# A hybrid attention and gated-MLP encoder layer: the rounded factors of w_down's first block are made among w_o's products, the first head's q and k are loaded earlier, and two pool results share one buffer

## The chip, the cores and the metric

The kernel runs on one core of a Trainium2 chip. The metric is the device time of one execution in microseconds (us): the median of the timed runs. A profiled execution beside them gives the trace; its span is a little shorter than its own time, since what lies around the first and the last instruction is not in it.

## The reference, cut to what matters

One layer over 512 tokens of width 2048, in float32. A combined projection gives q, k, v (eight heads of 128) and u (1024 channels for pooling); attention looks at its own chunk of 64 tokens and the eight before it, so with 512 tokens at everything up to the own chunk; the pool is a trailing mean minus the token, then a linear map per group. Then w_o, a residual, and a gated MLP with a depthwise causal convolution of three taps.

```python
h = rms_norm(x, pre_mix_g)
z = h @ w_in                                  # q | k | v | u
a = chunked_attention(q, k, v, rel_bias)
p = multiscale_pool(u, pool_w, pool_scale)    # windows 2, 4, 8, 16
x = x + rms_norm(concat(a, p) @ w_o, post_mix_g)
h = rms_norm(x, pre_ffn_g)
up = causal_dwconv(h @ w_up, conv_w, conv_b)
y = (gelu(up[..., :D_FF]) * up[..., D_FF:]) @ w_down   # D_FF = 5632
x = x + rms_norm(y, post_ffn_g)
```

## The kernel before, in words

**Split products.** TensorE multiplies rounded numbers (`fp32r`), so each float32 factor is split in two: ACT writes the rounded part (`hi`, line 140 or 143), DVE the rest (`lo = src - hi`, line 141 or 144). `split` does both. A product is then two or three matmuls (`mm3`, lines 162, 164, 165; `mm2`, lines 170 and 176). A weight is loaded into a raw buffer by SP, split into a pair of `w4` buffers, and read by TensorE. There are eight `w4` buffers, four pairs, given out in turn, and five shared raw buffers (`raw4`).

**Stages, in TensorE's order.** (1) Head 0's q and k, while x arrives. (2) `v_steps(0)`: half of v. (3) The projection of q and k of heads 1 to 7: k = 0 to 6, seven products each, named i = 1, 2, 5, 3, 6, 7, 4. It is Strassen's scheme in Winograd's form, seven products of halves instead of eight. Class `Pairs` holds the order, loads raw factors (`wx`, `ww`, `wz`, `wy`, line 449) up to eight products ahead and makes the split factors (`wfh`, `wfl`) up to four ahead. Product i = 4 adds onto the PSUM bank `qa` which ACT has just copied for i = 7 (`zm`, line 582), so TensorE waits there until ACT has read it. The finished z of each head is stored to DRAM (`zqk`, line 591). (4) Attention of heads 0 to 2 among the other half of v, then heads 3 to 7 among the eight u projections with the pool; each head loads its z into `zq` and its bias (`load_z`, `load_bias`), multiplies by the norm factor and splits it (`ready_head`) before `scores`. (5) w_o, again as seven products (`WO = 1, 7, 2, 5, 6, 3, 4`), each in two column halves `cc`, each half in four quarters of one weight pair. (6) The up projection, again in seven products per block: the longest part. (7) The down projection and the end.

**Side work.** The sums of weight blocks that Strassen's scheme needs for w_o and for the first block of w_down are made in DRAM by DMAs alone: copies and accumulating adds of 1 MB each, 48 in all (`sums_in_dram`; tensors `wt` and `t`). `more_sums(n)` issues the next n of them; calls stand at fixed places in the program. A paced one waits for a `pace` memset on DVE behind the last split. Besides, three factors of w_down's first block, (column half, product) = (0, 1), (1, 1), (0, 2), are rounded long before they are needed and kept in DRAM as `ready_w`; each is done in two parts, so there are six blocks of 512 KB. `Pairs` does that: one block behind product 7 of each of k = 0 to 5.

```python
v = self.raw[k, i] = p0.tile([P, 1024], F32, tag="rw", bufs=1, name="rw")   # line 455, loaded at 456
pair = w4("rwh"), w4("rwl")                                                 # line 474
split(*pair, self.raw.pop((k, i)))                                          # line 475
self.stores = [...]                                  # line 476; issued at the next make, line 468
```

The pair comes from the same four `w4` pairs as the factors that TensorE reads.

**Order.** TensorE's instructions stay as the program writes them. Those of ACT, DVE, POOL and SP are put in order when the kernel is built, by a scheduler with its own estimate of times; on the chip each of these engines works its list in order, and a waiting instruction holds all behind it. `tc.issue_after(ins)` puts an instruction behind another. The same layer places the tiles, and puts a wait before a buffer's next use. SP keeps at most eight of its DMAs on the way.

Of the kernel before, what the change touches and what calls it, by code (L numbers as in the profile page):

```python
# [9 lines left out]
F32 = mybir.dt.float32  # L10
# [71 lines left out]
def encoder_layer(ctx: ExitStack, tc: tile.TileContext, x, xT, vecs, rel, post_mix, post_ffn,  # L82
# [349 lines left out]
    class Pairs:  # L432
# [3 lines left out]
        def __init__(self):  # L436
# [6 lines left out]
            for m in range(len(ready_parts)):  # L443
                self.order.insert(self.order.index((m, 7)) + 1, (None, m))
            self.raw, self.made, self.loaded, self.used, self.stores = {}, [], 0, 0, []

        def load(self, k, i):
# [4 lines left out]
            if k is None:  # L452
# [5 lines left out]
            elif i == 1:  # L458
# [7 lines left out]
        def make(self, k, i):  # L466
            for dest, v in self.stores:
                nc.sync.dma_start(dest, f32(v).rearrange("p (a b) -> p a b", a=2))
            self.stores = []
            if k is None:  # L470
                if i is None:
                    weights.prefetch_to(FIRST_PART + 1)
                else:
                    (cc, n), j = ready_parts[i]
# [41 lines left out]
    for n, _ in enumerate(v_steps(0, psv)):  # L516
        if n in (4, 7, 10, 13):
            more_sums(1)
# [81 lines left out]
    steps = None  # L600
    for k, i in [at for at in pairs.order if at[0] is not None]:
# [11 lines left out]
        if i in ((3, 7, 4) if 0 < k < 5 else (7, 4)):  # L613
            more_sums(1)
# [10 lines left out]
    with tc.tile_pool(name="p1", bufs=2, reuse_waits="tile") as p1:  # L625
# [11 lines left out]
        t512("bias", bufs=1)  # L637
# [9 lines left out]

        state = {}
# [130 lines left out]
        load_z(0)  # L779
# [964 lines left out]
```

## Time and profile before

| | |
|---|---|
| median of 3 runs | 1921.48 us (1920.15 to 1921.66) |
| profiled execution | 1921.59 us, span 1919.8 us |
| busy, share of the span | PE 98%, PEld 83%, DVE 80%, ACT 56%, POOL 16% |
| HBM | 370.35 MB read, 104.33 MB written |
| DMA queues, share of 16 engines | q0 (POOL's) 44.8%, q1 (SP's) 37.9% |

A row of a timeline gives the start, the duration, the engine, the line, the operation, the tiles `out<-in`, and in brackets how long the engine had been idle before it and what ended that. A row of a table of waits gives who waited for whom, the total in us, how often, and the longest. A row of the chain of waits gives start, duration and what ran there. The DMA share is the mean busy share of the 16 DMA engines.

### The profile page before, as it was taken

What the parts mean: (1) busy time and instruction counts of PE and PEld (TensorE: products, weight loads), DVE (VectorE), ACT (ScalarE), POOL (GpSimd) and SP (SyncE); (2) the same over time, 40 slices, a digit from 0 to 9 for tenths busy, and PEclk for the clock granted to TensorE, in tenths of its full rate; (3) what the DMA queues carried; (4) which work ended last, traced back from release to release, by engine and by line L of the source; (5) the groups of instructions that cost most, each with busy time, mean ns of one, the idle gap of its engine ahead of it and who ended that gap; (6) DMA issues with size and microseconds to landing.
All of it is one profiled execution on the core that took longest, in us unless ns stands there. A gap on an engine that the chain in (4) does not pass through costs nothing.

```text
span 1919.8 us, 25463 instructions
## 1 busy us (share of the span) xinstructions
PE 1873.3 (98%) x9598; PEld 1595.0 (83%) x9598; DVE 1539.6 (80%) x1799; ACT 1080.7 (56%) x1376; POOL 299.0 (16%) x394
## 2 busy tenths in 40 slices
PE   9987879999999999999999999999999999999998
PEld 7876768788889888888888888888888888888886
DVE  6876657778678988888887888888887799898875
ACT  8544435446546566656565656556565665565553
POOL 3211010110000121222212121222211011111111
PEclk9998989999999999999999999999999999999999
DMA  7699997779967789898988888888988977877785
GB/s 258 211 265 289 288 260 242 186 211 277 351 203 291 181 210 211 195 204 194 210 197 199 203 202 208 196 204 194 206 189 274 349 226 176 197 198 169 173 229 152
DMA packets 140026, 426.01 MB, mean 222 GB/s; under 512 B 11968, under 2 KB 15424, under 8 KB 134208
## 3 DMA queue, kind: packets, MB, share of 16 engines
q0 software_dynamic: 54528, 170.41, 44.8%
q1 hardware_dynamic: 85376, 253.98, 37.9%
q8 instruction: 75, 1.23, 0.3%
q14 instruction: 47, 0.39, 0.1%
HBM read 370.35 MB, written 104.33 MB: 247 GB/s over the span
## 4 chain that ended last, share of the span: by engine, by line
PE 90%; DMA 5%; DVE 2%; ACT 2%; issue 1%; SPq 0%; DVEq 0%; ACTq 0%; POOLq 0%
PE qa L170 17%; PE qa L176 9%; PE qg L170 9%; PE qg L176 4%; PE qd L170 4%; PE pa L162 4%; PE pa L164 4%; PE pa L165 4%; PE m L164 3%; PE m L165 3%; PE m L162 2%; PE qd L176 2%; PE pg L162 2%; PE pg L164 2%; PE pg L165 2%; PE v L162 1%
## 5 line engine op out<-in xcount | busy, mean ns | idle before, releaser
L141 DVE TENSOR_TENSOR wfl<-wx,wfh 128x1024 fp32r<-128x1024 f32 x192 | 234.8, 1223 | 93.8 <-ACT wfh L140 70.5
L140 ACT ACTIVATE wfh<-wx 128x1024 fp32r<-128x1024 f32 x192 | 203.4, 1059 | 180.5 <-PE qg L170 50.7
L170 PE MATMUL qa<-gT,wfh 128*128 128x512 f32 x1152 | 295.7, 399 | 0.0
L170 PEld LDWEIGHTS qa<-gT,wfh 128*128 128x128 f32 x1152 | 212.1, 193 | 39.1
L176 PE MATMUL qa<-gT,wfl 128*128 128x256 f32 x1152 | 165.7, 288 | 21.8 <-ACT zm L582 21.4
L1361 POOL DMA_DIRECT2D wx<-in_w_up x122 | 104.5, 857 | 499.7 <-DVE wfl L141 476.8
L176 PEld LDWEIGHTS qa<-gT,wfl 128*128 128x128 f32 x1152 | 154.4, 194 | 27.8 <-ACT zm L582 22.7
L170 PE MATMUL qg<-h,wfh 128*128 128x512 f32 x656 | 165.7, 394 | 0.0
L140 ACT ACTIVATE wfh<-wy 128x1024 fp32r<-128x1024 f32 x96 | 101.8, 1060 | 110.2 <-PE qg L170 60.1
L170 PEld LDWEIGHTS qg<-h,wfh 128*128 128x128 f32 x656 | 122.9, 188 | 28.0
L141 DVE TENSOR_TENSOR bl<-b,bh 128x2048 fp32r<-128x2048 f32 x56 | 127.4, 2288 | 22.8 <-ACT bh L140 11.8
L140 ACT ACTIVATE bh<-b 128x2048 fp32r<-128x2048 f32 x56 | 105.8, 1912 | 48.1 <-DVE b L1119 20.3
L141 DVE TENSOR_TENSOR wfl<-wy,wfh 128x1024 fp32r<-128x1024 f32 x96 | 117.2, 1221 | 12.2 <-ACT wfh L140 4.0
L162 PE MATMUL pa<-bh,ah 128*128 128x512 f32 x320 | 126.1, 394 | 0.0
L164 PE MATMUL pa<-bl,ah 128*128 128x512 f32 x320 | 125.8, 393 | 0.0
L165 PE MATMUL pa<-bh,al 128*128 128x512 f32 x320 | 125.5, 392 | 0.0
L141 DVE TENSOR_TENSOR wfl<-wz,wfh 128x1024 fp32r<-128x1024 f32 x48 | 58.8, 1224 | 55.4 <-PE qa L170 53.5
L170 PE MATMUL qd<-gT,wfh 128*128 128x512 f32 x384 | 95.7, 391 | 0.0
L176 PEld LDWEIGHTS qg<-h,wfl 128*128 128x128 f32 x656 | 89.4, 188 | 7.5
L176 PE MATMUL qg<-h,wfl 128*128 128x256 f32 x656 | 91.6, 282 | 0.0
L170 PEld LDWEIGHTS qd<-gT,wfh 128*128 128x128 f32 x384 | 72.0, 188 | 16.2
L170 PE MATMUL qa<-h,wfh 128*128 128x512 f32 x328 | 83.2, 395 | 0.0
(549 smaller groups left out, 4363.5 us busy)
## 6 DMA issues: line engine op xcount, KB each, us to landing
wx<-in_w_up POOLq DMA_DIRECT2D x122, 512.0 KB, 5.9
b<-in_w_down SPq DMA_DIRECT2D x32, 1024.0 KB, 6.8
wt<-in_w_o POOLq DMA_DIRECT2D x24, 1024.0 KB, 14.8
wx<-in_w_up SPq DMA_DIRECT2D x43, 512.0 KB, 5.4
wz<-in_w_up SPq DMA_DIRECT2D x41, 512.0 KB, 5.7
wy<-in_w_up SPq DMA_DIRECT2D x41, 512.0 KB, 4.6
wy<-in_w_up POOLq DMA_DIRECT2D x41, 512.0 KB, 6.7
sum<-part POOLq DMA_DIRECT2D x38, 512.0 KB, 6.3
```

Of the source, the lines that this page charges most:

```text
L140: rounded = nc.scalar.activation(hi, src, AF.Copy)
L141: rest = nc.vector.tensor_sub(lo, src, f32(hi))
L162: nc.tensor.matmul(ps, l[0], r[0], start=first, stop=False, skip_group_check=onto)
L164: nc.tensor.matmul(low, l[0], r[1], start=False, stop=False, skip_group_check=onto)
L165: nc.tensor.matmul(ps, l[1], r[0], start=False, stop=last, skip_group_check=onto)
L170: nc.tensor.matmul(ps, w[0][:, kb], pairs[kb][0], start=fresh and not kb, stop=last, skip_group_check=not fresh)
L176: nc.tensor.matmul(ps[:, sl], w[1][:, kb], pair[:, sl], start=False, stop=last, skip_group_check=not fresh)
L1361: nc.gpsimd.dma_start(self.raw[k, what], self.block(k, m, kh), accum_op=ALU.add)
```

## The change

The six blocks leave the projection. `Pairs` no longer has entries for them. A generator `ready_block` does one block during each half of the w_o products 5, 6 and 3: it loads the block at the first quarter, splits at the third and stores both parts at the fourth. Its tiles `rw` and `rwh` belong to the pool `p2` of the w_o stage, one buffer each; the lower part is written in place over the raw block.

The 48 sums are issued at other places: 6 instead of 4 in `v_steps(0)`, 20 instead of 18 in the projection, 6 instead of 5 in heads 0 to 2, 6 as before in the middle of the u projections, 5 instead of 4 behind them, 3 instead of 9 among w_o's products, and 2 as before in the up projection.

Head 0's z and bias are loaded right after `restore` (called behind product 7 of k = 6) into two `raw4` buffers, no longer when `p1` has been opened. `bias` gets two buffers, and the later loads of z and bias are put behind the loads of `restore` or behind the last weight load.

`spill_mix` gathers two pool results in one `raw4` buffer and stores both with one DMA of 512 KB; before, each went through one 256 KB buffer `mx` of its own.

```diff
@@ class Pairs
             self.order.insert(-2, (None, None))
-            for m in range(len(ready_parts)):
-                self.order.insert(self.order.index((m, 7)) + 1, (None, m))
...
-                if i is not None:
-                    (cc, n), j = ready_parts[i]
-                    v = self.raw[k, i] = p0.tile([P, 1024], F32, tag="rw", bufs=1, name="rw")
-                    nc.sync.dma_start(v.rearrange("p (a b) -> p a b", a=2),
-                                      first_block(cc, n - 1, 0)[:, 2 * j:2 * j + 2, :])
...
-            for dest, v in self.stores:
-                nc.sync.dma_start(dest, f32(v).rearrange("p (a b) -> p a b", a=2))
-            self.stores = []
...
-                    pair = w4("rwh"), w4("rwl")
-                    split(*pair, self.raw.pop((k, i)))
-                    self.stores = [(dest[:, 2 * j:2 * j + 2, :], v) for dest, v in zip(ready_w[cc, n], pair)]
@@ v_steps(0)
-        if n in (4, 7, 10, 13):
+        if n in (3, 5, 7, 9, 11, 13):
             more_sums(1)
@@ the projection's loop
         if (k, i) == (pairs.n - 1, 7):
             restore()
-        if i in ((3, 7, 4) if 0 < k < 5 else (7, 4)):
+            state["z", 0] = raw4("zq0").rearrange("p (a b) -> p a b", a=2)
+            nc.sync.dma_start(state["z", 0], zqk[0])
+            state["bias", 0] = raw4("bias0")[:, :S]
+            restore.last = nc.sync.dma_start(state["bias", 0], rel[0]).ins
+        if i in ((3, 7, 4) if k < pairs.n - 1 else (7, 4)):
             more_sums(1)
@@ attention
-        t512("bias", bufs=1)
+        t512("bias", bufs=2)
...
         def load_bias(h):
-            state["bias", h] = t512("bias", bufs=1)
-            nc.sync.dma_start(state["bias", h], rel[h])
+            state["bias", h] = t512("bias", bufs=2)
+            with tc.issue_after(restore.last):
+                nc.sync.dma_start(state["bias", h], rel[h])
 
         def load_z(h):
             state["z", h] = p1.tile([P, 2, S], F32, tag="zq", bufs=1, name="zq")
-            nc.sync.dma_start(state["z", h], zqk[h])
+            with tc.issue_after(load_w.last if h == 1 else restore.last):
+                nc.sync.dma_start(state["z", h], zqk[h])
...
         def spill_mix(kb, ps, scale):
-            v = t512("mx", bufs=1)
-            nc.scalar.activation(v, ps, AF.Copy, scale=scale)
-            nc.sync.dma_start(pooled[:, kb - HEADS, :], v)
+            if kb % 2 == 0:
+                state["mx"] = raw4("mx").rearrange("p (a b) -> p a b", a=2)
+            nc.scalar.activation(state["mx"][:, kb % 2], ps, AF.Copy, scale=scale)
+            if kb % 2:
+                nc.sync.dma_start(pooled[:, kb - 1 - HEADS:kb + 1 - HEADS, :], state.pop("mx"))
...
-        load_z(0)
-        load_bias(0)
         v_load(0)
...
-            if h:
-                more_sums(1)
+            more_sums(1)
...
-                more_sums(1 if j % 2 or not j else 0)
+                more_sums(1 if j in (0, 1, 3, 5, 6) else 0)
@@ w_o
+        def ready_block(at, j):
+            v, hi = (p2.tile([P, 1024], dt, tag=tag, name=tag) for tag, dt in (("rw", F32), ("rwh", F32R)))
+            lo = v.bitcast(F32R)
+            nc.sync.dma_start(v.rearrange("p (a b) -> p a b", a=2), first_block(at[0], at[1] - 1, 0)[:, 2 * j:2 * j + 2, :])
+            yield
+            yield
+            split(hi, lo, v)
+            yield
+            for dest, part_ in zip(ready_w[at], (hi, lo)):
+                nc.sync.dma_start(dest[:, 2 * j:2 * j + 2, :], f32(part_).rearrange("p (a b) -> p a b", a=2))
+
         def wo_product(i, cc, left, between=None):
             ps = [bank(f"m{i}{cc}{t}") for t in range(2)]
-            if cc:
-                more_sums(2 if i in (3, 6) else 1)
+            if cc and i in (1, 5, 6):
+                more_sums(1)
+            ready = ready_block(*ready_parts.pop(0)) if i in (5, 6, 3) else iter(())
             for q in range(4):
...
+                next(ready, None)
```

Each fence shows one engine's instructions in the order in which they stand in the built kernel. First ACT, which makes the rounded parts, in the projection around the end of one k and the start of the next. Before (`qa`, a PSUM bank, copied into `zm` for product 7 is the last row; `rwh` is the block's rounded part):

```order
L140 ACTIVATE wfh<-wy 128x1024
L140 ACTIVATE rwh<-rw 128x1024
L568 ACTIVATE za<-qa_1227 128x512
L140 ACTIVATE wfh<-wx 128x1024
L578 ACTIVATE zm<-qa_1036 128x512
L140 ACTIVATE wfh<-wx 128x1024
L140 ACTIVATE wfh<-wy 128x1024
L140 ACTIVATE wfh<-wx 128x1024
L582 ACTIVATE zm<-qa_1036 128x512
```

and now:

```order
L140 ACTIVATE wfh<-wy 128x1024
L140 ACTIVATE wfh<-wx 128x1024
L551 ACTIVATE za<-qa_1222 128x512
L140 ACTIVATE wfh<-wx 128x1024
L561 ACTIVATE zm<-qa_1039 128x512
L140 ACTIVATE wfh<-wy 128x1024
L140 ACTIVATE wfh<-wx 128x1024
L565 ACTIVATE zm<-qa_1039 128x512
```

The row of `rwh` is gone, and the factors behind it have moved up by one place.

Second SP, which issues the loads, at the end of the projection. Before (`zqk` are the stored heads in DRAM, `u` and `v` weights):

```order
L152 DMA v_1r<-in_w_v 128x1024
L591 DMA zqk_352<-z 128x1024
L152 DMA v_2r<-in_w_v 128x1024
L152 DMA v_3r<-in_w_v 128x1024
L152 DMA u_0r<-in_w_u 128x1024
L152 DMA u_1r<-in_w_u 128x1024
L591 DMA zqk_353<-z 128x1024
L667 DMA zq<-zqk_346 128x1024
L663 DMA bias<-in_rel 128x512
```

and now:

```order
L152 DMA v_1r<-in_w_v 128x1024
L574 DMA zqk_352<-z 128x1024
L597 DMA zq_2029<-zqk_346 128x1024
L599 DMA bias_2031<-in_rel 128x512
L649 DMA bias<-in_rel 128x512 x2
L152 DMA v_2r<-in_w_v 128x1024
L654 DMA zq<-zqk_347 128x1024
L574 DMA zqk_353<-z 128x1024
```

Head 0's load has moved up past two v weights, two u weights and the store of the last head.

Third the w_o stage, where the blocks are now. ACT before, at the end of product 2's weights and the start of product 5's (`wo_1_…` is a quarter of the second column half, `wo_0_…` of the first):

```order
L140 ACTIVATE s_4634<-mixT_3915 128x1024
L140 ACTIVATE s_4634<-mixT_3916 128x1024
L140 ACTIVATE wo_1_0h<-wo_1_0r 128x1024
L140 ACTIVATE wo_1_1h<-wo_1_1r 128x1024
L140 ACTIVATE wo_1_2h<-wo_1_2r 128x1024
L140 ACTIVATE wo_1_3h<-wo_1_3r 128x1024
L140 ACTIVATE wo_0_0h<-wo_0_0r 128x1024
```

and now:

```order
L140 ACTIVATE rwh<-rw 128x1024
L140 ACTIVATE s_4616<-mixT_3885 128x1024
L140 ACTIVATE wo_1_0h<-wo_1_0r 128x1024
L140 ACTIVATE s_4616<-mixT_3886 128x1024
L140 ACTIVATE wo_1_1h<-wo_1_1r 128x1024
L140 ACTIVATE wo_1_2h<-wo_1_2r 128x1024
L140 ACTIVATE wo_1_3h<-wo_1_3r 128x1024
L140 ACTIVATE rwh<-rw 128x1024
L140 ACTIVATE wo_0_0h<-wo_0_0r 128x1024
```

Blocks two and three stand ahead of `wo_1_0h` of product 2 and `wo_0_0h` of product 5; block four, six rows on, ahead of `wo_1_1h` of product 5. SP there, now, with what each row waits for (the rows from `wt_96` are product 5's):

```order
L846 DMA rw01l<-rw 128x1024 [waits DMAHW3_49,DMAHW1_49]
L152 DMA wo_1_1r<-in_w_o 128x2x512 [waits DMAHW2_49,DVE_49]
L840 DMA rw<-in_w_down 128x2x512 [waits DMAHW1_49]
L152 DMA wo_1_2r<-in_w_o 128x2x512 [waits DMAHW4_49,DVE_49]
L152 DMA wo_1_3r<-in_w_o 128x2x512 [waits DMAHW5_49,DVE_49]
L152 DMA wo_0_0r<-wt_96 128x1024 [waits DMAHW6_49,DMAHW7_49,DMASW4_49,DVE_49]
L846 DMA rw01h<-rwh 128x1024 [waits Activation_49]
L846 DMA rw01l<-rw 128x1024 [waits DMAHW3_49,DMAHW0_49,DVE_49]
L152 DMA wo_0_1r<-wt_96 128x1024 [waits DVE_49]
L152 DMA wo_0_2r<-wt_96 128x1024 [waits DMAHW2_49,DMASW5_49,DVE_49]
L840 DMA rw<-in_w_down 128x2x512 [waits DMAHW0_49]
L152 DMA wo_0_3r<-wt_96 128x1024 [waits DMAHW4_49,DVE_49]
```

The blocks' loads stand further ahead than the program writes them, the second already among product 2's weights. Each load but the first waits for the DMA that stored the lower part of the block before it out of the same tile (`DMAHW…`), and weights of w_o are queued behind it.

More of the change, by code (lines that the diff above doesn't have):

```diff
@@ L442, in __init__ @@
             self.order.insert(-2, (None, None))
-            for m in range(len(ready_parts)):
-                self.order.insert(self.order.index((m, 7)) + 1, (None, m))
-            self.raw, self.made, self.loaded, self.used, self.stores = {}, [], 0, 0, []
+            self.raw, self.made, self.loaded, self.used = {}, [], 0, 0
         def load(self, k, i):
@@ L466, in make @@
         def make(self, k, i):
-            for dest, v in self.stores:
-                nc.sync.dma_start(dest, f32(v).rearrange("p (a b) -> p a b", a=2))
-            self.stores = []
             if k is None:
[L471 to L474, printed above, removed]
-                    pair = w4("rwh"), w4("rwl")
-                    split(*pair, self.raw.pop((k, i)))
-                    self.stores = [(dest[:, 2 * j:2 * j + 2, :], v) for dest, v in zip(ready_w[cc, n], pair)]
+                weights.prefetch_to(FIRST_PART + 1)
                 self.made.append(None)
```

6 lines of the change are left out of this document (2 added, 4 removed).

## The prediction

> **What bounds the kernel now.** I read the page's slices first, then TensorE's waits over the whole span, then two stretches of the same kind of work.
>
> ```profile
> PEclk9998989999999999999999999999999999999999
> PE qa L176 <- ACT zm L582: 21.4, 6, 5.8
> PE s L162 <- ACT qkh L140: 11.0, 2, 9.8
> PE m L164 <- DVE wo_3l L141: 1.0, 1, 1.0
> 102.00:231.00 129.00, 110.10 (x568) 95.17 (x569) 87.80 (x109) 54.97 (x69) 15.86 (x30) 0.90 0.96 276
> 700.00:1400.00 700.00, 699.70 (x3992) 612.59 (x3991) 578.22 (x680) 423.82 (x520) 149.44 (x178) 1.00 0.87 202
> ```
>
> The first row is TensorE's granted clock in 40 slices, the next three are waits (total, times, longest). The last two are stretches: their length, busy time of PE, PEld, DVE, ACT and POOL, the granted clock, the DMA engines' share, GB/s. TensorE sets the end: in 700 us of the up projection, the same seven products, it is never free. In the projection of q and k it lacks 19 of 129 us, the granted clock is 0.90, and the DMA engines are full. What can be won lies there and in the two waits ahead of scores.
>
> The six waits name ACT's copy `zm`, but ACT itself was held by a DMA. One of them, from the chain of waits (start, duration) and the timeline, and ACT's own waits:
>
> ```profile
> 137.83 13.06 DMA rw11h<-rwh
> ...
> 150.97 1.06 ACT L140 ACTIVATE wfh<-wx 128x1024 fp32r<-128x1024 f32 x1 [10.11 <-DMA rw11h<-rwh]
> 153.83 0.57 ACT L582 ACTIVATE zm<-qa 128x512 f32<-128x512 f32 x1
> 154.46 2.08 PE L176 MATMUL qa<-gT,wfl 128*128 128x256 f32 x8 [5.79 <-ACT zm L582]
> ...
> ACT wfh L140 <- DMA rw11h<-rwh: 18.4, 2, 10.1
> ACT wfh L140 <- DMA rw01h<-rwh: 14.7, 2, 8.4
> ```
>
> The block's rounded part keeps one of the four `w4` pairs until its store has landed, here 13.06 us after its issue. The next factor for that pair waits in ACT's list, and behind it the copy that frees the bank. Six blocks, six waits.
>
> **What leaves the path.** The chain gives the period with the stall and without:
>
> ```profile
> 103.64 2.05 PE L176 MATMUL qa<-gT,wfl 128*128 128x256 f32 x8 [4.13 <-ACT zm L582]
> 229.62 1.79 PE L176 MATMUL qa<-gT,wfl 128*128 128x256 f32 x8 [2.38 <-ACT zm L582]
> ...
> 231.41 2.83 PE qa L170 x8
> 706.59 1.89 PE qa L176 x16
> 708.48 1.87 PE qa L170 x8
> 1020.57 1.89 PE qa L176 x16
> ```
>
> Clean, 16 times the work of one k lies between the two rows of `x16`: (1020.57 - 706.59) / 16 = 19.62 us for one k. Stalled: (229.62 - 103.64) / 5 = 25.20. Five periods lose 5 x 5.58 = 27.9. The first wait, 4.13, lies ahead of them, and behind the last one the matmuls still run slow: 1.79 + 2.83 against 1.89 / 2 + 1.87, so 1.8. Together **33.8 us**. Without the block's row in ACT's list no store stands between factor and copy.
>
> By the Trainium skill's page "TensorE: Matmul & The Clock Gate", section "Why this matters for your kernels", the clock drops once TensorE idles for more than about 3 us. The wait ahead of 229.62 is 2.38 us and is followed by slow matmuls too, so here the trace goes further than the page; by the page the 1.8 would be no cost of that wait, and the sum 32.0.
>
> *Head 0.* Its z is loaded last of all on SP and lands late; TensorE waits and then runs slow (head 1's score matmuls for comparison):
>
> ```profile
> 253.81 12.66 DMA zq<-zqk
> ...
> 241.24 0.33 SPq L152 DMA_DIRECT2D v_2r<-in_w_v  x1
> 268.87 0.58 PE L162 MATMUL s<-qkh 128*128 128x256 f32 x1 [9.75 <-ACT qkh L140]
> 270.13 0.58 PE L164 MATMUL s<-qkl,qkh 128*128 128x256 f32 x1 [0.68 <-DVE qkl L141]
> 271.36 0.52 PE L162 MATMUL s<-qkh 128*128 128x384 f32 x1
> 273.60 0.63 PE L162 MATMUL v<-v_6h,gT 128*128 128x512 f32 x1
> ...
> 286.73 0.34 PE L162 MATMUL s<-qkh 128*128 128x384 f32 x1
> 287.95 0.39 PE L162 MATMUL v<-v_0h,gT 128*128 128x512 f32 x1
> ```
>
> 9.75 + 0.68 of waits. The last six score matmuls take 2.24 us against 1.22; the first six lose about as much, and the v matmuls behind them 0.4: 2.5 in all. Together **12.9**. Now `zq0` takes the raw buffer that `v_2r` got at 241.24. Even with today's 12.66 us it lands at 253.9; multiplying and splitting took 270.1 - 266.5 = 3.6 us, so it is ready at 257.5, and TensorE gets there at 268.87 - 9.75 = 259.1. Cover: 1.6 us; if it lands 5 us later still, 3.4 of the 12.9 come back. What is pushed back on SP are `v_2` and `v_3`: v is taken in the order 4 to 7, 0 to 3, and `v_0` is only being multiplied at 287.95, so they have over 30 us.
>
> *Pool results.* The second `mx` copy waits in ACT's list for the store of the first:
>
> ```profile
> 363.79 6.21 DMA pooled<-mx
> 431.81 8.00 DMA pooled<-mx
> ...
> 377.28 0.98 PE L722 MATMUL pt<-ident,s 128*128 128x128 f32 x7 [1.11 <-DVE pace L295]
> 379.50 0.39 PE L162 MATMUL s<-qkh 128*128 128x256 f32 x1 [1.25 <-ACT qkh L140]
> 380.76 0.58 PE L164 MATMUL s<-qkl,qkh 128*128 128x256 f32 x1 [0.88 <-DVE qkl L141]
> ```
>
> These three waits make 3.24 and, at the rate just seen, 1.6 of slow matmuls; the chain leads from them to the first store, and from the wait of `m` (1.0) to the second. Two copies into one buffer need no store between them. Between 0 and 5.8; I take **5**, since the chain has nothing else of that length in its way. The new buffer is out of the weights' ring until its 512 KB have landed; u weights are loaded two parts of 24 matmuls ahead, 11 us, more than the 8.00.
>
> Sum: 33.8 + 12.9 + 5 = 51.7 us.
>
> **What is added.** *More sums in the projection*, 20 for 18. All are POOL's, which waits for `pace` and not for time; their first reader is product 7 of w_o. The cost is the DMA engines' time (76 to 260 us; packets, MB, share of 184 us):
>
> ```profile
> q1 hardware_dynamic: 10223, 31.66, 48.4%
> q0 software_dynamic: 6652, 19.33, 44.0%
> zqk<-z SPq DMA_DIRECT2D x7, 512.0 KB, 8.6
> ```
>
> SP's queue takes 184 x 0.484 / 31.66 = 2.81 us per MB, POOL's 4.19. A k needs five transfers of 0.524 MB, 7.4 us, and three sums of 1.05 MB, 13.2: 20.6 us against TensorE's 19.62. From the other side: 0.96 of 25.2 less one block (1.57 MB, 4.4) is 19.8. So the engines stay as full as they are. Lower bound 0: a backlog of 6 x 1.0 us delays no reader. Upper bound: the engines set the pace at their 0.96, (20.6 / 0.96 - 19.62) x 6 = 11 us. Factors are loaded up to eight products ahead, 22 us of TensorE's time, and a transfer of their size lands in about 8.6 (third row); so nearer to 0: I take **3**.
>
> *The blocks among w_o's products.* Six more splits of 1.06 us on ACT and 1.2 on DVE, for which both have room (first row below). The risk is a wait: block n + 1 may be loaded only when the lower part of block n has landed, and its split stands in ACT's list ahead of weights.
>
> ```profile
> 472.00:530.00 58.00, 58.00 (x258) 48.02 (x257) 41.89 (x38) 35.06 (x41) 2.30 (x2) 1.00 1.01 349
> 469.93 0.67 ACT L768 ACTIVATE mixT<-pm,vec 128x512 f32<-128x512 f32 x1
> 522.88 0.60 ACT L895 ACTIVATE y<-m 128x512 f32<-128x512 f32 x1 [1.21 <-PE m L165]
> 533.76 0.60 ACT L895 ACTIVATE y<-m 128x512 f32<-128x512 f32 x1 [1.21 <-PE m L165]
> DMA to landing us min/median/max: 6.6/14.9/17.0
> wo_1r<-wt SPq DMA_DIRECT2D x4, 512.0 KB, 5.7
> ```
>
> On today's clock the first load can go at about 472.5, when the pool's last product has left its tiles. A block takes load l, split 2.3, store s. The fourth block's split is then at 472.5 + 3 (l + 2.3 + s) + l, and the weight behind it, `wo_1_1` of product 5, is split 3.5 us later. Half a product is 533.76 - 522.88 = 10.9 us; product 5, whose first half is copied out at 522.88, begins at 512.9 and wants that weight 10.9 + 2.7 later, at 526.6. It is late by 4 l + 3 s - 43.7. For l there are 5.7 (w_o's weights there), 6.6 (the least of the block's own six loads) and 14.9 (their median in the full projection); for s 6.21 (half the size) to 13.06. Six sums leave this stage, so I take 6.6 and 6.21: late by 1.3, with slow matmuls **2 us**; with 5.7 not at all; the upper ends are rivals (b) and (c).
>
> The sums added in v, the heads and u stand beside an idle POOL (2.30 of 58.00 us above, 15.86 of 129) and cost nothing; without that cover each is its issue, about 1 us.
>
> 51.7 - 3 - 2 = 46.7. The sum is made against the profiled execution's 1921.59 us (span 1919.8), 0.1 above the median: 1874.9, so **1875 us**.
>
> **The rivals.** (a) *The DMA engines become the bound of the projection*: 11 us as above, and a backlog that makes head 0's z and v's weights late, 9 at most: 1921.6 - 51.7 + 2 + 11 = 1883, to 1892. For it: the share of 0.96. Against: the up projection runs at 0.87 without a wait. By the Trainium skill's page "DMA: Bandwidth & Descriptors", section "Queues, rings and completion order", each engine takes turns between the queues packet by packet, so SP's loads, which need 38% of a period, would not suffer from POOL's backlog; no run shows that yet. (b) *w_o gives part back*: l and s both at 8.6, the `zqk` store's, make it late by 16.5, with 4 of slow matmuls: 1921.6 - 51.7 + 3 + 20.5 = 1893. For it: the share of 1.01 there. Against: 5.7. (c) *Slower*: the same chain with the projection's l = 14.9 and s = 13.06 is late by 55, with slow matmuls 60: 1921.6 - 51.7 + 3 + 60 = 1933. It decides from 4 l + 3 s = 90 on; against it speaks that w_o's loads land in less than half of that. (d) *The change doesn't do what it says*: ACT then waits in the projection for loads where it waited for stores, and the six stalls stay; only head 0 and the pool are won, 1904, or nothing, 1921.
>
> **How the numbers follow.** Forecast, 1867 to 1879: 0.61. (a) 0.17, (b) 0.11, (c) 0.04, (d) 0.04, more than all known waits 0.03. The range 1867 to 1897 holds the forecast, (a) and (b): 0.89, and the likeliest has most of it. A measurement of this kernel tells 0.2% (3.8 us) from no change: faster 0.94, the same 0.02, slower 0.04.
>
> **What would show it.** No wait of ACT's `wfh` for a `rw` store and none of `qa` for `zm` in the projection; its k at 19.6 to 20.2 us, the granted clock near 1.00 from 100 to 250; head 0's score matmuls right behind v; no copy `mx` waiting for `pooled`. In w_o, ACT's `rwh` waiting up to 8 us for the load of `rw`, and a short wait of `m` for `wo_0_0` or `wo_1_1` at product 5. I am wrong if the projection's period stays above 21 us, or if TensorE waits more than 5 us in w_o.

## The result, and the profile after

The changed kernel takes 1878.41 us (median of 4 runs, 1876.19 to 1881.62) against 1920.83 us for the kernel before (4 runs, 1920.15 to 1921.66): ratio 0.978, 95% interval 0.9763 to 0.9797. The prediction was 1875 us, range 1867 to 1897. The profiled execution of the changed kernel is the slowest of its four, 1881.62 us with a span of 1879.9 us.

From its page, the busy time of the engines:

```profile
PE 1860.0 (99%) x9598; PEld 1584.6 (84%) x9598; DVE 1539.7 (82%) x1805; ACT 1082.1 (58%) x1376; POOL 303.3 (16%) x403
```

The two slices of 8 have gone from the row of TensorE's granted clock, which reads 9 in all 40. To see where the 39.9 us between the two spans lie, I take the starts of four kinds of matmul that open a stage: the first scores, the first u projection, the first product of w_o, the first matmul of the up projection. From the groups of TensorE's instructions by tile (shortest, median and longest in ns, first and last start in us), the kernel before:

```profile
L162 PE MATMUL s<-qkh x32: 277/364/628, 268.9 to 399.1; 128*128 128x256 f32 x16, 128*128 128x384 f32 x8, 128*128 128x512 f32 x8
L162 PE MATMUL u<-gT,u_0h x64: 387/389/501, 315.0 to 437.0; 128*128 128x512 f32 x64
L162 PE MATMUL m<-wo_0h,a x16: 389/389/389, 443.1 to 503.6; 128*128 128x512 f32 x16
L162 PE MATMUL up<-gT,w_0h x32: 278/376/396, 603.0 to 656.3; 128*128 128x256 f32 x16, 128*128 128x512 f32 x16
```

and the changed kernel:

```profile
L162 PE MATMUL s<-qkh x32: 278/339/632, 226.3 to 354.7; 128*128 128x256 f32 x16, 128*128 128x384 f32 x8, 128*128 128x512 f32 x8
L162 PE MATMUL u<-gT,u_0h x64: 387/389/505, 275.0 to 392.6; 128*128 128x512 f32 x64
L162 PE MATMUL m<-wo_0h,a x16: 389/389/389, 398.7 to 457.9; 128*128 128x512 f32 x16
L162 PE MATMUL up<-gT,w_0h x32: 279/376/396, 560.7 to 615.0; 128*128 128x256 f32 x16, 128*128 128x512 f32 x16
```

| stretch | before | after | difference | in the prediction's terms |
|---|---|---|---|---|
| start to first scores | 268.9 | 226.3 | -42.6 | -33.8 - 9.75 + 3 = -40.6 |
| scores to u | 46.1 | 48.7 | +2.6 | -0.68 - 2.5 = -3.2 |
| u to w_o | 128.1 | 123.7 | -4.4 | -4 |
| w_o to up projection | 159.9 | 162.0 | +2.1 | +2 - 1 = +1 |
| up projection to end | 1316.8 | 1319.2 | +2.4 | 0 |
| sum | | | -39.9 | -46.8 |

So the projection and head 0's wait gave a little more than forecast, and two places gave something back that was not in the sum: the heads (5.8 us) and the last stretch (2.4 us). What TensorE waited for in the changed kernel, of the same view as shown for the kernel before:

```profile
PE s L162 <- DVE ptl L141: 3.8, 1, 3.8
PE qa L176 <- ACT zm L1420: 1.7, 2, 0.9
PE up L162 <- DVE gT L144: 1.0, 1, 1.0
PE m L164 <- DVE wo_0l L141: 0.9, 1, 0.9
PE m L162 <- ACT wo_0h L140: 0.3, 1, 0.3
```

The projection has no wait left. The 3.8 us are new. The chain of waits names their source, and ACT's timeline shows how it reaches TensorE (second fence):

```profile
221.18 20.77 DMA v_3r<-in_w_v
```

```profile
242.02 1.06 ACT L140 ACTIVATE v_3h<-v_3r 128x1024 fp32r<-128x1024 f32 x1 [5.39 <-DMA v_3r<-in_w_v]
242.99 1.23 ACT L140 ACTIVATE pth<-pt 128x512 fp32r<-128x512 f32 x3
```

v's weight `v_3r` lands 20.77 us after its issue, and its split stands in ACT's list ahead of `pth`, the copy of head 0's turned scores that frees the banks for head 1's. TensorE stands there although it needs v_3 itself only later (its first matmul with `v_3h` starts at 268.5).

### The profile page after: what moved, and what is told of

It reads as the page before. It is cut to its first block, busy times and chain, and to the rows that moved or that the text cites. A ratio compares the mean times of both kernels' runs of the same rounds, so it can differ in the third digit from the quotient of the medians.

```text
span 1879.9 us, 25452 instructions
## 1 busy us (share of the span) xinstructions
PE 1860.0 (99%) x9598; PEld 1584.6 (84%) x9598; DVE 1539.7 (82%) x1805; ACT 1082.1 (58%) x1376; POOL 303.3 (16%) x403
## 3 DMA queue, kind: packets, MB, share of 16 engines
q0 software_dynamic: 54864, 173.56, 46.1%
## 4 chain that ended last, share of the span: by engine, by line
PE 88%; DMA 4%; DVE 4%; ACT 2%; issue 1%; SPq 0%; POOL 0%; DVEq 0%; POOLq 0%; ACTq 0%
PE qa L170 18%; PE qa L176 9%; PE qg L170 9%; PE qg L176 5%; PE qd L170 4%; PE pa L162 4%; PE pa L164 4%; PE pa L165 4%; PE qd L176 2%; PE pg L162 2%; PE pg L164 2%; PE pg L165 2%; PE m L164 2%; PE m L165 2%; PE m L162 2%; PE u L162 1%
## 5 line engine op out<-in xcount | busy, mean ns | idle before, releaser
L170 PE MATMUL qa<-gT,wfh 128*128 128x512 f32 x1152 | 289.1, 393 | 0.0
L141 DVE TENSOR_TENSOR wfl<-wx,wfh 128x1024 fp32r<-128x1024 f32 x192 | 234.7, 1223 | 64.0 <-ACT wfh L140 46.7
L170 PEld LDWEIGHTS qa<-gT,wfh 128*128 128x128 f32 x1152 | 207.0, 188 | 37.5
L176 PE MATMUL qa<-gT,wfl 128*128 128x256 f32 x1152 | 160.8, 282 | 1.7 <-ACT zm L1420 1.7
L141 DVE TENSOR_TENSOR bl<-b,bh 128x2048 fp32r<-128x2048 f32 x56 | 127.3, 2287 | 22.5 <-ACT bh L140 11.7
L140 ACT ACTIVATE bh<-b 128x2048 fp32r<-128x2048 f32 x56 | 105.8, 1912 | 49.2 <-DVE b L1118 20.5
```

What stands on the lines that cost most here:

```text
L140: rounded = nc.scalar.activation(hi, src, AF.Copy)
L141: rest = nc.vector.tensor_sub(lo, src, f32(hi))
L170: nc.tensor.matmul(ps, w[0][:, kb], pairs[kb][0], start=fresh and not kb, stop=last, skip_group_check=not fresh)
L176: nc.tensor.matmul(ps[:, sl], w[1][:, kb], pair[:, sl], start=False, stop=last, skip_group_check=not fresh)
```

## The experiments

Runs of one kernel here differ by 1 to 9 us (head 0 alone: 1910.14 to 1916.64), so parts of a few us are read from the stage starts as well as from medians. For the projection the measure is its period: product 2 is the only one that writes the bank `qd`, so its first matmuls come once for each k. The two rows of TensorE's timeline lie five k apart; first the kernel before, then the changed one:

```profile
90.61 2.00 PE L170 MATMUL qd<-gT,wfh 128*128 128x512 f32 x8
...
218.63 2.01 PE L170 MATMUL qd<-gT,wfh 128*128 128x512 f32 x8
```

```profile
91.45 2.00 PE L170 MATMUL qd<-gT,wfh 128*128 128x512 f32 x8
...
190.21 2.01 PE L170 MATMUL qd<-gT,wfh 128*128 128x512 f32 x8
```

### Which half of the block stalls the projection: the held pair or its bytes?

**Own tile.** In the kernel before, the rounded part goes to a small tile of its own instead of a `w4` pair:

```diff
...
-                    pair = w4("rwh"), w4("rwl")
-                    split(*pair, self.raw.pop((k, i)))
-                    self.stores = [(dest[:, 2 * j:2 * j + 2, :], v) for dest, v in zip(ready_w[cc, n], pair)]
+                    own = p0.tile([P, 512], F32R, tag="rwh", bufs=1, name="rwh")
+                    split(own, own, self.raw.pop((k, i))[:, :512])
+                    self.stores = [(dest[:, 2 * j:2 * j + 2, :], own) for dest in ready_w[cc, n]]
```

> The kernel before, with the six blocks left in the projection and the same bytes moved for them; only the rounded tile is no pair of the `w4` ring but a small tile of its own (its first half alone is split, so 0.5 us of ACT and 0.6 us of DVE are left out for each block, and what is stored are not the right values). Theory (a pair of the ring is held until its store has landed): ACT's `wfh` no longer waits for a `rw` store, the projection's period falls from 25.2 to 19.6 to 21 us, and the time from 1921 to 1887 to 1893 us. Rival (the DMA engines set the projection's pace): one k still needs five transfers of 7.4 us, three sums of 13.2 and a block of 4.4, together 25.0 us of DMA time, so the period stays at 24 to 25 us and the time at 1915 to 1921 us. Between 1897 and 1910 both have a part.

Measured: 1920.52 us (11 runs), ratio 1.0 (0.9991 to 1.0009): nothing won. ACT's waits in the projection, and the longest but one in its timeline:

```profile
ACT rwh L140 <- DMA rw<-in_w_down: 36.1, 6, 8.6
```

```profile
132.88 0.63 ACT L140 ACTIVATE rwh<-rw 128x512 fp32r<-128x512 f32 x1 [8.13 <-DMA rw<-in_w_down]
```

The waits for stores are gone, as meant, but the block's load has taken their place, six times, with the same `zm` right behind it (here at 133.42). The scheduler had also moved `rwh` further ahead. The time would fit the rival, but the test did not separate the two: it exchanged one late transfer in front of ACT for another.

**Other source.** A cleaner cut: the block is split into its pair as before and ACT's list stays almost as it was, but the stores read a tile that stands ready.

```diff
-            for dest, v in self.stores:
-                nc.sync.dma_start(dest, f32(v).rearrange("p (a b) -> p a b", a=2))
+            for dest in self.stores:
+                with tc.issue_after(load_w.last):
+                    nc.sync.dma_start(dest, f32(ms[5][:, :2]).rearrange("p a b c -> p a (b c)"))
...
```

> The kernel before; the six blocks are loaded and split into a `w4` pair in the projection as before, and ACT's list is almost the same, but the two stores of a block read another tile that stands ready (the same bytes, the wrong values), so the pair is free as soon as it is split. The first test of this left a load in the way: ACT's `rwh` waited 36 us for `rw`. Theory (the hold of the pair until its store lands is the stall): no ACT wait behind a store, period 19.6 to 21.5 us, time 1887 to 1897 us. Rival 1 (with a block's bytes the DMA engines need 25.0 us for one k and set the pace): period 24 to 25, time 1915 to 1921 us. Rival 2 (one full queue always gives one late transfer in front of ACT; with the store gone it is the block's load): ACT's `rwh` waits for `rw` 15 us or more in all, period 22 to 24, 1900 to 1912 us.

Measured: 1903.83 us, ratio 0.991 (0.9896 to 0.9923). Half of the 33.8 us came, half did not. TensorE's timeline and ACT's waits:

```profile
90.39 2.00 PE L170 MATMUL qd<-gT,wfh 128*128 128x512 f32 x8
...
112.48 2.01 PE L170 MATMUL qd<-gT,wfh 128*128 128x512 f32 x8
...
151.85 2.01 PE L170 MATMUL qd<-gT,wfh 128*128 128x512 f32 x8
173.04 2.01 PE L170 MATMUL qd<-gT,wfh 128*128 128x512 f32 x8
195.85 2.01 PE L170 MATMUL qd<-gT,wfh 128*128 128x512 f32 x8
```

```profile
ACT wfh L140 <- DMA wz<-in_w_qk: 12.2, 3, 5.3
ACT rwh L140 <- DMA rw<-in_w_down: 5.7, 3, 2.2
```

The mean period is (195.85 - 90.39) / 5 = 21.09 us, but it is not even: the first is 22.1, two run at the clean 19.7, then come 21.2 and 22.8, with ACT waiting for the factors' own loads. None of the three is right as it stands. The theory's period (19.6 to 21.5 us) is met in the mean, but its time is missed; the factors' loads then come late, but rival 1's 24 to 25 us are not reached; and the time lies in rival 2's range, but its wait for `rw` is only 5.7 us of the 15 it names.

**Traffic.** The other half by itself: the changed kernel, in which no block is in the projection, with only the blocks' bytes put back there. A load and two stores of 512 KB for each k go through SP, and no engine waits for them.

```diff
...
+            for dest in self.stores:
+                with tc.issue_after(load_w.last):
+                    nc.sync.dma_start(dest, f32(ms[5][:, :2]).rearrange("p a b c -> p a (b c)"))
+            self.stores = []
...
+                    self.stores = self.scratch
```

> The changed kernel with the blocks' bytes put back into the projection and nothing else of them: for each of k = 0 to 5 one load of 512 KB and two stores of 512 KB on SP's queue, which no engine waits for (they come on top; the blocks in w_o stay). One k then needs five transfers of 7.4 us, three sums of 13.2 and 4.4 for these, 25.0 us of DMA time. Theory (the engines' share is no bound as long as no in-order engine stands behind a late transfer): period 19.7 to 20.5 us, time 1878 to 1886 us, the sums land later. Rival (the DMA engines set the pace): period 24 to 25 us, time 1905 to 1912 us.

Measured: 1898.14 us (1897.69 to 1899.69), 19.7 more than the changed kernel. TensorE's timeline, ACT's waits, and the DMA issues (KB each, median us to landing):

```profile
91.47 2.01 PE L170 MATMUL qd<-gT,wfh 128*128 128x512 f32 x8
...
209.80 2.01 PE L170 MATMUL qd<-gT,wfh 128*128 128x512 f32 x8
```

```profile
ACT wfh L140 <- DMA wz<-in_w_qk: 18.3, 5, 5.6
```

```profile
wz<-in_w_qk SPq DMA_DIRECT2D x5, 512.0 KB, 17.5
```

The period is (209.80 - 91.47) / 5 = 23.67 us. No block and no held pair is there; the bytes alone cost 3.9 us for each k. The theory, as put on record, has fallen. The rival's ranges (24 to 25 us, 1905 to 1912 us) are not met either, but nearly.

**Extra copy.** The same DMA time, on the other queue:

```diff
...
+        def extra():
+            for v in scratch:
+                copy(v, first_block(0, 1, 0))
+                yield
...
+        if i == 2 and k < pairs.n - 1:
+            next(extra_step[0])
```

> The changed kernel with one more copy of 1 MB from DRAM to DRAM on POOL's queue in each of k = 0 to 5, into a place that nobody reads. It takes 4.4 us of DMA time for one k, as much as the block's bytes took on SP's queue, where they cost 20 us (1898 us) since the factors' loads landed after 13 to 17.5 us instead of 7 to 10. Theory (any byte more on the full engines makes the factors' loads late, whichever queue it is on): the same 25.0 us of DMA time for one k, factors' loads after 13 us or more, time 1894 to 1900 us. Rival (the queues take turns, and SP's own backlog alone made its loads late): SP's loads land as in the changed kernel (7 to 10 us), POOL's copies after 25 us or more, time 1878 to 1885 us.

Measured: 1890.09 us (1887.95 to 1891.42), 11.7 more than the changed kernel, between the two. In the projection the rival is right to the letter; its time, 1878 to 1885 us, is missed:

```profile
90.62 2.01 PE L170 MATMUL qd<-gT,wfh 128*128 128x512 f32 x8
...
189.16 2.02 PE L170 MATMUL qd<-gT,wfh 128*128 128x512 f32 x8
```

```profile
wz<-in_w_qk SPq DMA_DIRECT2D x5, 512.0 KB, 9.5
scratch<-in_w_down POOLq DMA_DIRECT2D x6, 1024.0 KB, 27.1
```

Period 19.71 us: SP's loads land as in the changed kernel (there 9.8), POOL's copies after 27.1. The bill comes behind it: the backlog runs on into the heads, where SP wants more.

```profile
240.41 22.54 DMA zq<-zqk
```

| kernel | projection's period, us | SP's DMA time for one k | POOL's | time |
|---|---|---|---|---|
| before | (218.63 - 90.61) / 5 = 25.60 | 7.4 + 4.4 | 13.2 | 1921 |
| own tile | (220.32 - 92.33) / 5 = 25.60 | 7.4 + 4.4 | 13.2 | 1920.5 |
| other source | 21.09, last one 22.8 | 7.4 + 4.4 | 13.2 | 1903.8 |
| traffic | 23.67 | 7.4 + 4.4 | 13.2 | 1898.1 |
| extra copy | 19.71 | 7.4 | 13.2 + 4.4 | 1890.1 |
| changed | (190.21 - 91.45) / 5 = 19.75 | 7.4 | 13.2 | 1878.4 |
| sums back (below) | (189.76 - 91.34) / 5 = 19.68 | 7.4 | 13.2 | 1880.0 |
| blocks back (below) | (226.77 - 90.60) / 5 = 27.23 | 7.4 + 4.4 | 13.2 | 1918.1 |

The theory that takes the place of the fallen one has two parts. First, SP's bytes. An estimate from the prediction's prices: if SP's queue gets about half of the engines while POOL's always has work, one k with the block's bytes takes 2 x 11.8 = 23.6 us, measured 23.67 in traffic and 22.8 in the last k of other source; without them it is 2 x 7.4 = 14.8, under TensorE's 19.62. Traffic alone doesn't tell this from a bound by the engines' whole time, since 25.0 us at the two queues' measured share, 0.492 + 0.555 = 1.05, make 23.8. The extra copy does: at the same share, 0.391 + 0.659, the same 25.0 us leave the period at 19.71, and POOL's queue alone falls behind. Packets, MB and share of the 16 engines from 76 to 250 us, in traffic and then in the extra copy:

```profile
q0 software_dynamic: 8555, 24.10, 55.5%
q1 hardware_dynamic: 10337, 31.95, 49.2%
```

```profile
q0 software_dynamic: 10150, 30.19, 65.9%
q1 hardware_dynamic: 7776, 25.29, 39.1%
```

The half itself stays an estimate. The Trainium skill's page "DMA: Bandwidth & Descriptors", section "Queues, rings and completion order", has each engine take turns between queues packet by packet; the landing times of the extra copy (9.5 and 27.1 us) agree with it.

Second, a late transfer in front of ACT, store or load, comes on top. With the sums of the kernel before, one k takes 19.68 us without the blocks (sums back), 21.09 with their bytes (other source) and 25.60 with the held pair too. With the sums of the changed kernel it takes 19.75, 23.67 (traffic) and 27.23 (blocks back). So the held pair costs 4.5 and 3.6 us for each k, the bytes 1.4 and 3.9. Why the bytes cost more with the changed kernel's sums was not tested by itself; it issues two more of them ahead of the projection and one more behind k = 0.

### The parts one by one

**Blocks back.** The changed kernel with the blocks again in `Pairs` and in `w4` pairs, by the lines that the change took out (sums at the new places).

> The changed kernel with one part undone: the six blocks go back to the projection and to a `w4` pair (the sums stay at the changed kernel's places, 20 in the projection). Theory (the term of 33.8 us, less 2 for w_o): the six stalls return, period 25 to 26 us, the time is 1878 + 32 = 1910 us (1905 to 1914). Rival (most of the projection's stall came from its DMA traffic, which the changed kernel has nearly the same of): 1880 to 1895 us.

Measured: 1918.09 us (11 runs), ratio to before 0.9985 (0.9975 to 0.9994). Undoing the blocks costs 39.7 us, not 32.

```profile
90.60 2.00 PE L170 MATMUL qd<-gT,wfh 128*128 128x512 f32 x8
...
226.77 2.01 PE L170 MATMUL qd<-gT,wfh 128*128 128x512 f32 x8
```

The same six waits of `qa` for `zm`, longer (27.0 us in all against 21.4 before), and a period of 27.23 us against 25.60. The sums' places are all that differs from the kernel before up to there: with the blocks in the projection they cost 1.6 us for each k, without them 0.07 (19.75 against 19.68). So the parts are not additive, and moving the blocks is what made room for the sums.

**Head 0 alone**, in the kernel before, by the diff's lines on `zq0`, `bias0` and `issue_after` (the bias of later heads keeps one buffer).

> The kernel before with one part of the change: head 0's z and bias are loaded early into raw buffers (the bias of later heads keeps one buffer). Theory (the term of 12.9 us): the waits of 9.75 and 0.68 us before head 0's scores and the slow matmuls go, the time is 1908 us (1905 to 1911). Rival (the raw buffers and the place on SP's queue taken from v's weights come back as a wait behind head 0, as the 3.82 us of the changed kernel suggests): 1912 to 1916 us, with a wait of head 1's scores that the kernel before doesn't have.

Measured: 1912.7 us, ratio 0.996 (0.9947 to 0.9973), 8.4 us of 12.9. The first scores start at 256.9, 12.0 earlier, the first u at 305.0, 10.0 earlier. The waits name what is late next, and the chain its source:

```profile
PE pt L726 <- DVE s L715: 3.7, 3, 1.7
```

```profile
252.27 14.70 DMA zq<-zqk
...
270.66 13.37 DMA zq<-zqk
```

The rival has the right kind, a wait behind head 0, but at another transfer: not v's weights but z of heads 1 and 2.

**Pool results alone**, `spill_mix` of the diff in the kernel before.

> The kernel before with one part of the change: two pool results share one raw buffer and one store. Theory (the term of 5 us): no copy `mx` waits for `pooled`, the three waits at 377 to 381 us (3.2 us) and one of 1.0 us in w_o go, the time is 1916 us (1914 to 1918). Rival (the waits pass to something else, such as the weights that lose a raw buffer): 1919.5 to 1922 us, with waits of the same size for another tile within 30 us.

Measured: 1912.43 us, ratio 0.9959 (0.9946 to 0.9973), 8.7 us. From u to w_o it takes 435.2 - 312.6 = 122.6 us against 128.1, from w_o to the up projection 158.7 against 159.9: 6.7 us that belong to the edit. From 300 to 700 us TensorE waits for nothing any more. The time lies below the theory's range, so the term is somewhat larger than 5; 6.7 is from one profile, and the interval of the ratio reaches from 5.2 to 10.4 us.

**Sums back**, the changed kernel with its 48 sums at the places of the kernel before.

> The changed kernel with the 48 sums at the places of the kernel before (18 instead of 20 in the projection, 5 instead of 6 in heads 0 to 2, 9 instead of 3 in w_o). Theory (3 us for more sums in the projection, and the late `v_3r` from their backlog): the 3.8 us wait of head 1's scores is gone or under 1 us, but the sums among w_o's products make the blocks' transfers there later; time 1874 to 1880 us. Rival (the sums had to leave w_o for the blocks to fit): TensorE waits 5 us or more in w_o, time 1883 us or more. If the sums cost nothing anywhere, 1878 within 2.

Measured: 1880.04 us (1878.74 to 1885.13), ratio 0.9791 (0.9775 to 0.9808): not told apart from the changed kernel. Theory and rival were each right in part. The wait of head 1's scores is gone and the u projection starts 4.3 us earlier (270.7); but w_o takes 167.2 instead of 162.0 us, with waits of 5.1 us in it and at its end. What the sums cost in one place they cost in the other.

### Better versions

**Late sums.**

```diff
...
-        if i in ((3, 7, 4) if k < pairs.n - 1 else (7, 4)):
+        if i in ((3, 7, 4) if k < pairs.n - 1 else ()):
...
-            more_sums(1)
+            if h:
+                more_sums(1)
...
-                more_sums(1 if j in (0, 1, 3, 5, 6) else 0)
+                more_sums(1)
...
-            if cc and i in (1, 5, 6):
+            if cc and i in (1, 5, 6, 3):
```

> The changed kernel with four sums moved away from the end of the projection and head 0 (two behind k = 6, one in head 0; now two more among the u projections and one more in w_o). Theory (POOL's copies beside `v_3r` make it land after 20.8 us, and v_3's split stands in ACT's list ahead of head 0's `pth`): `v_3r` lands within 13 us, the wait of 3.8 us and its slow matmuls go, time 1872 to 1876 us. Rival (SP's own transfers, q0, v, u and `vl`, are what fills the engines there): `v_3r` still lands after 17 us or more, time 1877 to 1880 us.

Measured: 1877.88 us (1877.71 to 1879.65). `v_3r` lands after 8.4 us, the wait is gone, u starts at 269.0 instead of 275.0: the cause of the 3.8 us is shown, and that they were worth 6 us. But w_o waits:

```profile
PE m L164 <- DVE wo_0l L141: 2.0, 3, 0.9
```

Five such groups, the largest shown, make 5.0 us; w_o takes 168.1 us instead of 162.0, and all is given back. (The text on record says four sums; three were moved.)

**Spread blocks**, one block to a product of w_o instead of two:

```diff
-            ready = ready_block(*ready_parts.pop(0)) if i in (5, 6, 3) else iter(())
+            ready = ready_block(*ready_parts.pop(0)) if i != 1 and not cc else iter(())
```

> The changed kernel with the six blocks in w_o one to a product instead of two: in the first half of products 7, 2, 5, 6, 3 and 4, so 21.8 us apart instead of 10.9. A block's chain of load, split and store takes 5.5 + 2.3 + 3.4 us here, up to 8.8 + 2.3 + 7.9. Theory (the term of w_o: the next load waits for the store of the last block, and weights stand behind it): TensorE's two waits at product 5 (0.33 and 0.95 us) and their slow matmuls go, time 1875 to 1878 us, 1 to 3 us less. Rival (these waits come from the weights' own loads beside the full engines): waits of `m` of 1 us or more in all remain, time 1878 to 1881 us.

Measured: 1875.44 us (1874.48 to 1875.89), ratio to before 0.9766 (0.9753 to 0.978). No `m` waits any more. All four runs lie below all four of the changed kernel, 3.0 us by the medians; the intervals of the two ratios overlap. It is the best version found, below both kernels.

**Spread blocks, and the sums in the up projection** (label `best`, the name given before it ran):

```diff
...
+            if i == 3 and k % 2:
+                more_sums(1)
```

in the loop of the seven products, with the calls behind the u projections, in w_o and at the end of the projection taken out.

> A version made from what the runs showed: the changed kernel with the blocks one to a product in w_o, and with the sums moved off the full stretches: none behind k = 6 nor first in head 0, none behind the u projections or in w_o, and 13 of the 16 sums of w_down's block spread over the up projection of seven products (one every second block; they are read at 1425 us). Theory: the 3.8 us wait of head 1's scores with its slow matmuls (6.0 us by the start of the u projection), w_o's 2 us and the 2.4 us lost at the start of the up projection go: 1868 to 1873 us. Rival (POOL's own adds of factors there are held up by the sums): waits of `qa` or `qg` in the up projection, time 1877 to 1890 us.

Measured: 1896.17 us, 17.8 more than the changed kernel. Up to the up projection all came as expected (it starts at 553.5, 7.2 earlier). In it:

```profile
PE qg L170 <- ACT zb L1413: 17.7, 9, 2.9
```

```profile
952.45 2.02 PE L170 MATMUL qg<-h,wfh 128*128 128x512 f32 x8
960.45 2.83 PE L170 MATMUL qg<-h,wfh 128*128 128x512 f32 x8 [2.23 <-ACT zb L1413]
...
1003.71 2.12 PE L170 MATMUL qg<-h,wfh 128*128 128x512 f32 x8 [2.23 <-ACT zb L1413]
```

```profile
946.48 12.27 DMA wx<-in_w_up
```

A factor's add on POOL's queue, 6.6 us in the changed kernel (median), takes 11.88 (at 905.15) and 12.27 behind a sum of 1 MB. The rival has the mechanism, and the cost is above its range of 1877 to 1890: up to here POOL had seemed to be free.

**Combined.** Spread blocks, with the three sums elsewhere:

```diff
...
-                more_sums(1)
+                more_sums(2 if h in (3, 4) else 1)
...
-            if cc and i in (1, 5, 6):
+            if cc and i in (1, 2, 5, 6):
```

> The changed kernel with the blocks one to a product in w_o (1875 us by itself, 3 less) and three sums moved from the end of the projection and head 0 (1878 by itself: 6 us won by the start of u, as much lost in u and w_o, where they went behind the u projections' tails); here two go to the middle of the third and fourth u projection, where the DMA engines' share was 0.65 to 0.78, and one into product 2 of w_o. Theory (what is lost depends on where the queue is full when a load is wanted): both gains stay, no wait of head 1's scores, waits in w_o under 1 us in all, time 1869 to 1873 us. Rival (a sum costs about the same wherever it goes before w_o ends): 1874 to 1877 us.

Measured: 1876.03 us (1873.41 to 1879.27), the same as spread blocks alone. u starts at 269.1, 2.8 us before that of spread blocks, the up projection at 556.2 in both: what the heads win, u and w_o lose. That is the rival's 1874 to 1877.

## Why the prediction was right, and where it was not

*The projection, 33.8 us.* The size was right, the step behind it was only part of the cause: "without the block's row in ACT's list no store stands between factor and copy" was taken for the whole. With the pair freed and the bytes left (other source), 17.4 of the 33.8 us came. In one k the held pair makes 25.60 - 21.09 = 4.5 us and the bytes the rest, 1.4; with the changed kernel's sums the bytes are the larger part, 3.9 against 3.6. More is lost behind the fifth k: by the first scores other source is 20.0 us ahead of the kernel before, the changed kernel 42.6, of which 9.75 are head 0's. The 33.8 were read off as stalled period less clean period, which holds every cause, named or not, and the change removes both. That is why the sum came out, and to that extent it was luck: had the change removed only the hold, the forecast would have been wrong by 16 us with the old sums (other source) and by 20 with the new ones (traffic).

*Sums in the projection, 3 us, bounds 0 to 11.* Measured 5 x (19.75 - 19.62) = 0.7 there, and sums back has 19.68. The upper bound set the engines' total time against their share of 0.96 and asked nothing of queues; extra copy has the same 25.0 us of DMA time as traffic and no longer period. In the changed kernel the share itself reads above 1 while TensorE is never free, so it is no measure of how much room is left:

```profile
150.00:175.00 25.00, 25.00 (x145) 21.87 (x144) 20.22 (x25) 12.39 (x16) 1.93 (x6) 1.00 1.07 317
```

*"A backlog of 6 x 1.0 us delays no reader"* was wrong, *"so they have over 30 us"* (`v_2` and `v_3`) looked at the wrong reader, and this is the main miss. `v_3r` has over 40 us until TensorE wants it, but only 15 until ACT's list comes to its split (issued at 220.8, split at 236.2, first matmul at 262.5 in late sums, where no scores wait), with head 0's `pth` behind it. It cost 5.8 us in the heads; without the wait (late sums) they take 43.0 us, 3.1 less than before, where the sum had 3.2. Rival (a) had v's weights late by a backlog, 9 us at most, but not the place in ACT's list.

*Head 0, 12.9 us.* Won to the first scores; its 3.2 us behind them were covered by that new wait. The 1.6 us of cover held: head 0's scores follow v without a wait.

*Pool results, 5 us.* Mechanism right, size low: 6.7 by itself in the profile, 4.4 from u to w_o in the changed kernel.

*Blocks in w_o, 2 us.* Right in size and in mechanism. The stretch from w_o to the up projection is 2.1 us longer, where 2 - 1 was forecast; 1.0 of it is a wait of `up` that stands ahead of its first matmul (below), so 1.1 against 1. The chain of waits shows the link that the formula is made of, a load that starts when the store of the block before it has landed:

```profile
439.02 7.03 DMA rw01l<-rw
446.07 0.50 DMA rw<-in_w_down
```

The first four splits start at 435.08, 451.02, 465.20 and 478.59 us, 13.4 to 15.9 apart, where the formula has 6.6 + 2.3 + 6.21 = 15.1. ACT stood 7.43 us ahead of the third block's split, and `wo_0h` was next in its list:

```profile
465.20 1.06 ACT L140 ACTIVATE rwh<-rw 128x1024 fp32r<-128x1024 f32 x1 [7.43 <-issue]
```

So TensorE's wait, 0.33 and 0.95 us, came at `wo_0_0` of product 5, one block earlier than the formula's. With the blocks spread it is gone, so the blocks were its cause; which transfer came late at the third block the trace doesn't name.

*Start of the up projection.* No step had this. The first matmul of `up` waits 1.0 us for `gT`:

```profile
560.71 0.36 PE L162 MATMUL up<-gT,w_0h 128*128 128x256 f32 x1 [1.01 <-DVE gT L144]
```

A wait of `up` for `gT` is there in every run with the blocks in w_o and in none with them in the projection. Why is open.

*The last stretch, 2.4 us.* TensorE waits there for `zm` (L1420, 1.7 us in the table of waits) at 672.73 and 693.38 us, behind transfers of `wx` of 9.92 and 10.15 us, and its matmuls behind the two waits are slower. In the other runs with the blocks in w_o, `best` left out, these waits are 0.2 us at most, and the stretch takes 1316.8 to 1317.6 us against 1316.8 before. The profiled execution is the slowest of four; so most of the 2.4 us belongs to it and not to the change.

Of the rivals, (b), (c) and (d) did not occur. The forecast of 46.7 us stands against 42.4 by the medians and 40.0 by the profiled executions. By the medians the late `v_3r` alone, 6 us by late sums, is more than the difference.

## What to carry to other kernels

When an in-order engine waits for a DMA, ask two things apart: what its place in the list holds up, and which queue's bytes make the transfer late; taking away one of the two gives only its part. Price bytes by queue, not by the engines' sum: a queue that may lag behind costs nothing until its backlog meets a stretch where the other needs the engines. And the deadline of a load is the moment when the engine that splits it comes to it, with whatever stands behind in that list.

## What the hardware showed that was not expected

Two queues with the same added DMA time, 4.4 us for one k, gave a period of 23.67 us (SP's) and 19.71 us (POOL's). In the second, SP's transfers of 512 KB landed after 9.5 us (`wz`) in the projection and after 22.54 us (`zq`) in the heads, where POOL's backlog runs on and SP's queue holds more; which of the two did it was not tested.

Matmuls can run at about two thirds of their speed behind a wait, but the length of the wait alone doesn't decide it. In `best`, eight matmuls of `qg` take 2.02 us where nothing waits; behind two waits of 2.23 us they take 2.83 and 2.12 (the rows 952.45, 960.45 and 1003.71 above), behind one of 2.47 us (at 875.87) 3.48, and behind one of 2.85 us (at 675.92) 2.12. The granted clock was 0.71 from 960.4 to 963.3 us and 1.00 from 1003.7 to 1006. The Trainium skill's page "TensorE: Matmul & The Clock Gate", section "Why this matters for your kernels", speaks of gaps over about 3 us; these waits are shorter, and the measurement decides.
